# Opening loads in order of use on one queue, and parts of one bank for the mixers' small products, in a two-layer decoder trunk

## The chip, the cores and the metric

The kernel runs on one core of one Trainium2 chip. A core has five engines with instruction streams of their own: PE (TensorE, matrix products; its weight loads are listed apart as PEld), DVE (VectorE), ACT (ScalarE), POOL (GpSimd, used here to issue transfers) and SP (SyncE, which only issues transfers). An engine runs its stream in order; engines wait for one another by semaphores. A transfer that is issued on SP, ACT or POOL goes through that engine's queue, in order, and is issued only when the tile that it fills is free, so one that waits holds back all behind it. The metric is the device time of one execution in microseconds (us), lower is better. Times come as medians of several executions; a profile is one execution more, taken by the hardware profiler.

## The reference

Two layers over 256 tokens of width 1024, batch 1, float32, then a final RMS norm. Each layer is two half-step SwiGLU blocks around a token mixer; every one of the three has its own shift, scale and gate, computed from a vector c:

```
c_act = silu(c)
for l in 0, 1:
    mod = c_act @ w_ada[l] + b_ada[l]        # nine vectors of 1024: shift, scale, gate for each of three blocks
    h = rmsnorm(x, g[l,0]) * (1 + sc0) + sh0
    x = x + 0.5 * g0 * ((silu(h @ w_gate) * (h @ w_up)) @ w_down)          # inner width 2816
    h = rmsnorm(x, g[l,1]) * (1 + sc1) + sh1
    x = x + g1 * token_mix(h)
    h = rmsnorm(x, g[l,2]) * (1 + sc2) + sh2
    x = x + 0.5 * g2 * swiglu(h)             # a second set of weights
x = rmsnorm(x, final_g)
```

`token_mix` projects h to thirteen parts and joins three groups before an output projection: a gated MLP (gelu, a group norm, a causal 128x128 product), a differential attention with four heads (two softmax maps, one subtracted from the other), and a sparse attention with eight heads (compressed blocks of 32 tokens with a softmax over 15 of them, a selection of blocks, and a window).

## The kernel before

**Products.** x is held transposed as `xT`, 8 chunks k of 128 features by 256 tokens. A float32 product is made of three products of a shorter type: a weight tile `wst` (mostly 128x1024, 512 KB) is loaded by SP (L205), ACT rounds it to `wh` (L211), DVE takes the rest `wl = wst - wh` (L215), the activations are split likewise into a hi and a lo half of `h` (L279, L280), and PE adds wh by hi, wh by lo and wl by hi (L223, a helper that records all such products). `wst` has 5 buffers, `wh` and `wl` 6 each. PE has 8 banks of PSUM for results: 5 with tag "mm", 2 with tag "w", 1 with tag "st".

**Modulation.** w_ada is read in tiles `ast` of 128x1024 (512 KB, four buffers), loaded by POOL's queue (L181, and L374 in the opening). One DVE instruction multiplies a tile with the row `crow` = silu(c) and sums it into a column of 128 values (L192, in the opening L381). 16 tiles are due in the opening (scale and shift for each k); the other 128 are spread over the rest, and each must be summed before its block.

**The opening, `startup`.** The first SwiGLU starts with its first 7 column blocks of gate and up side by side: for every k a tile with 4 blocks (128x1024) and one with 3 (128x768) of `w_first`, products into 7 banks at once (`ps_fst`, 42 products per k). In the same loop stand the two `ast` sums for k+1, from which DVE makes `gs` (L383) and `mod` (L385), the scale and shift of one chunk, then `tn` (L276), and ACT and DVE make the halves of h. The first k is recorded in an order by hand for PE, DVE and ACT; the rest is laid out by a scheduler. In the whole loop the rest of the constants (`cst`, 706 KB, and `par`, 499 KB) and a small weight (`w2` from cmp_w2, 192 KB) are loaded on SP where the scheduler puts them. What follows is `ffn`: for the blocks 7 to 21 a gate and an up tile each (`ps_ws`), silu by ACT (`sg`, L344) times up by DVE (`a`, L349), then the down products (`ps_dn`), which DVE adds to `xT` (L332) and turns into `ut` (L294), the input of the mixer's first projections (`ps_wu`).

**The mixers.** `mix` runs a list of named steps, MIX_ORDER, whose order is PE's order; the other engines' orders are laid out by the scheduler, which puts an instruction where it sees its engine free. In the list of layer 0, `a` is `ada_step`: sum two tiles, load two. Projections (`ws_in`) take the two banks of tag "w"; so do the two products `xs_in` that come before them, and DVE copies half of these away (`dv`, L655) ahead of the first projection's use of the bank. Three small results take turns in the one bank "st": `ps_cs` (scores of the compressed blocks), `ps_ct` (their probabilities transposed) and `ps_da` (the norm of the differential attention).

Of the kernel before, what the change touches and what calls it, by code (L numbers as in the profile page):

```python
# [112 lines left out]
def trunk_kernel(ctx: ExitStack, tc: tile.TileContext, A, depth=DEPTH, nf=NF, fsplit=FSPLIT):  # L113
# [93 lines left out]

    def split(src, cols, mid=None):
        st = load(src, cols)
        wh = whp.tile([P, cols], F32R, name="wh", tag="wh")  # L210
        nc.scalar.activation(wh, st, AF.Copy)  # L211
# [151 lines left out]
    def startup(ns):  # L363
# [3 lines left out]
        nc.gpsimd.dma_start(crow, A["crow"])  # L367
        b1 = sm.tile([P, KD], F32, name="b1", tag="b1", bufs=1)

        def ada_load0(k):  # L370
            sts = []
            for m in (1, 0):
                st = adp.tile([P, D], F32, name="ast", tag="ast")
                nc.gpsimd.dma_start(st, A["w_ada"][0, m, k])  # L374
                sts.append(st)
            return sts

        def ada_sum0(k, sts):
            red = sm.tile([P, 2], F32, name="red", tag="red")
            for n, st in enumerate(sts):  # L380
                nc.vector.scalar_tensor_tensor(out=st, in0=st, scalar=1.0, in1=crow, op0=ALU.mult, op1=ALU.mult,  # L381
                                               accum_out=red[:, n:n + 1])
            nc.vector.scalar_tensor_tensor(out=gs[0][:, 0, k:k + 1], in0=red[:, 0:1], scalar=b1[:, k:k + 1],  # L383
                                           in1=lp(0, "ng")[:, k:k + 1], op0=ALU.add, op1=ALU.mult)
            nc.vector.tensor_add(mod[0][:, 0, k:k + 1], red[:, 1:2], lp(0, "bada")[:, k:k + 1])  # L385

        def first(k, mid=None):
            parts = []
            for f0, f1 in ((0, (ns + 1) // 2), ((ns + 1) // 2, ns)):
                if f1 > f0:  # L390
                    src = A["w_first"][k, :, f0 * 2 * P:f1 * 2 * P]
                    parts.append((f0, f1, *split(src, 2 * (f1 - f0) * P, None if f0 else mid)))
            return parts

        with tc.manual_schedule(engines={mybir.EngineType.PE, mybir.EngineType.DVE, mybir.EngineType.Activation}):
# [24 lines left out]
            ada_sum0(0, sts)  # L420
            rb = rms_bcast(rsqrt_tokens(st), in_psum=True)
            parts = first(0, lambda: h_chunk(0, 0, 0, rb))
        pss = []
        for f in range(ns):
            pool_, tag = (psm, "mm") if f < 5 else (psw, "w")
            pss.append(pool_.tile([P, 2 * T], F32, name="ps_fst", tag=tag))
        for k in range(KD):
            if k:
                parts = first(k)
            if k + 1 < KD:  # L430
                ada_sum0(k + 1, ada_load0(k + 1))
                h_chunk(0, 0, k + 1, rb)
            for f0, f1, wh, wl in parts:
                tiles = [(pss[f][:, e * T:(e + 1) * T], 2 * (f - f0) + e) for f in range(f0, f1) for e in range(2)]
                step = len(tiles) if k == 0 else 1
                for n0 in range(0, len(tiles), step):
                    for o, n in tiles[n0:n0 + step]:
                        s = slice(n * P, (n + 1) * P)
                        mm(o, wh[:, s], h[:, k, :T], start=(k == 0 and n % 2 == 0), stop=False)
# [695 lines left out]
```

## Time and profile before

| what | value |
|---|---|
| three runs | 1076.78, 1077.12, 1075.27 us; median 1076.78 |
| profiled execution | 1076.35 us, of which the span from first to last instruction 1074.4 us; mean granted clock of TensorE 0.982 |
| busy | PE 1028.0 us (96%), DVE 849.0 (79%), ACT 576.3 (54%), POOL 77.7 (7%) |
| transfers | 258.05 MB, 240 GB/s on average |
| first product of the opening | at 17.66 us |
| first of the products that follow it (`ps_ws`) | at 73.20 us |
| mixer of layer 0, first product to the first of the next block | 215.94 to 361.79 us |
| mixer of layer 1, the same | 737.32 to 877.02 us |

A median of executions is compared with a median. The profiled execution's time lies 1.95 us above its span, since the span counts from the first instruction to the last. PE's busy time counts overlapped products, so 96% is not 96% of its peak; the granted clock tells how fast it was allowed to run (1.00 is full speed, near 0.50 is half).

### The profile page before, as it was taken

The numbers are of one execution on the slowest core, as the hardware profiler recorded it, in microseconds if no ns is written. First come the engines' busy times: TensorE is split into PE (matmuls) and PEld (weight loads), VectorE is DVE, ScalarE is ACT, GpSimd is POOL, SyncE is SP. The second block draws the span as 40 slices with busy tenths as digits, with TensorE's granted clock in tenths as the row PEclk, the third lists the DMA queues.
The fourth block names the chain that finished last, engine by engine and source line by source line (L and its number), as shares of the span: only waits on it lengthen the run. The fifth ranks groups of instructions, "written<-read, shape, count | busy, mean of one in ns | idle before, by whom it ended". The sixth has DMA issues, their size and how long they took to land.

```text
span 1074.4 us, 19840 instructions
## 1 busy us (share of the span) xinstructions
PE 1028.0 (96%) x7684; PEld 948.5 (88%) x7684; DVE 849.0 (79%) x1589; ACT 576.3 (54%) x1022; POOL 77.7 (7%) x151
## 2 busy tenths in 40 slices
PE   7789999999898999999999999999998999999997
PEld 5689998888676999998899999889786799999986
DVE  5689989989994899965679999667987489655553
ACT  4355544565576755444565544455566676444441
POOL 2101111000100022100001111000000001000000
PEclk8899999999999999999999999999998999999999
DMA  9899998947620499986658999765632057756551
GB/s 361 301 327 328 390 365 308 366 132 249 228 95 21 157 388 408 404 274 174 192 159 308 409 408 368 249 189 176 237 133 67 1 177 299 229 181 184 170 154 40
DMA packets 73967, 258.05 MB, mean 240 GB/s; under 512 B 8337, under 2 KB 9745, under 8 KB 73873
## 3 DMA queue, kind: packets, MB, share of 16 engines
q1 hardware_dynamic: 52560, 180.17, 48.7%
q0 software_dynamic: 20880, 76.03, 19.0%
q8 instruction: 60, 0.98, 0.4%
q10 hardware_dynamic: 432, 0.58, 0.2%
q14 instruction: 35, 0.28, 0.1%
HBM read 255.70 MB, written 1.05 MB: 239 GB/s over the span
## 4 chain that ended last, share of the span: by engine, by line
PE 77%; DVE 11%; DMA 6%; ACT 3%; issue 2%; POOL 0%; DVEq 0%; ACTq 0%; POOLq 0%; SPq 0%
PE ps_ws L223 42%; PE ps_dn L223 23%; PE ps_out L223 4%; PE ps_wu L223 4%; DVE wl L215 3%; DMA ast<-in_w_ada_dram 2%; PE ps_y L223 1%; DMA wst<-in_w_first_dram 1%; PE ps_s L223 1%; ACT pn L541 1%; DVE rt L515 1%; DVE mx L536 1%; DMA wst<-in_w_in_vs_dram 1%; ACT wh L211 1%; DVE h L280 1%
## 5 line engine op out<-in xcount | busy, mean ns | idle before, releaser
L211 ACT ACTIVATE wh<-wst 128x1024 fp32r<-128x1024 f32 (+2 forms) x332 | 342.0, 1032 | 360.7 <-issue 129.7
L215 DVE TENSOR_TENSOR wl<-wst,wh 128x1024 fp32r<-128x1024 f32 (+2 forms) x332 | 392.6, 1187 | 117.6 <-ACT wh L211 115.7
L223 PE MATMUL ps_ws<-h,wh 128*128 128x256 f32 x2720 | 481.3, 281 | 4.0 <-DVE dv L655 1.7
L223 PEld LDWEIGHTS ps_ws<-h,wh 128*128 128x128 f32 x2720 | 416.3, 189 | 7.4 <-DVE dv L655 2.5
L223 PE MATMUL ps_ws<-h,wl 128*128 128x256 f32 x1360 | 382.0, 281 | 0.0
L223 PEld LDWEIGHTS ps_ws<-h,wl 128*128 128x128 f32 x1360 | 261.1, 192 | 0.0
L223 PE MATMUL ps_dn<-act,wh 128*128 128x512 f32 (+1 forms) x726 | 247.9, 390 | 0.0
L223 PE MATMUL ps_dn<-act,wl 128*128 128x256 f32 x704 | 197.6, 281 | 0.0
L223 PEld LDWEIGHTS ps_dn<-act,wh 128*128 128x128 f32 x726 | 134.8, 188 | 30.8
L192 DVE SCALAR_TENSOR_TENSOR ast<-ast,crow 128x1024 f32<-128x1024 f32 x128 | 156.8, 1226 | 1.6 <-DMA ast<-in_w_ada_dram 1.6
L223 PEld LDWEIGHTS ps_dn<-act,wl 128*128 128x128 f32 x704 | 133.1, 189 | 0.0
L181 POOL DMA_DIRECT2D ast<-in_w_ada_dram x128 | 68.0, 531 | 465.3 <-DVE ast L192 144.2
L223 PE MATMUL ps_wu<-ut,wh 128*128 128x258 f32 (+1 forms) x320 | 60.1, 286 | 0.8 <-DVE ut L294 0.8
L223 PE MATMUL ps_fst<-h,wh 128*128 128x256 f32 x224 | 42.1, 300 | 12.6 <-ACT h L279 12.6
L223 PEld LDWEIGHTS ps_wu<-ut,wh 128*128 128x128 f32 x320 | 49.9, 189 | 1.4 <-DVE ut L294 1.3
L223 PEld LDWEIGHTS ps_fst<-h,wh 128*128 128x128 f32 x224 | 36.5, 208 | 14.1 <-ACT h L279 13.8
L223 PE MATMUL ps_out<-y,wh 128*128 128x256 f32 x256 | 47.3, 286 | 0.4 <-DVE xT L332 0.4
L219 ACT ACTIVATE act<-a 128x256 fp32r<-128x256 f32 x88 | 35.6, 412 | 18.3 <-DVE a L349 17.0
L223 PE MATMUL ps_wu<-ut,wl 128*128 128x258 f32 x160 | 45.2, 283 | 0.0
L349 DVE TENSOR_TENSOR a<-ps_ws,sg 128x256 f32<-128x256 f32 x75 | 32.0, 427 | 14.8 <-PE ps_ws L223 14.8
L223 PEld LDWEIGHTS ps_out<-y,wh 128*128 128x128 f32 x256 | 39.8, 191 | 2.0 <-issue 1.0
L332 DVE SCALAR_TENSOR_TENSOR xT<-ps_dn,hg,xT 128x256 f32<-128x256 f32 x63 | 30.4, 482 | 12.6 <-PE ps_dn L223 11.5
(202 smaller groups left out, 1033.0 us busy)
## 6 DMA issues: line engine op xcount, KB each, us to landing
ast<-in_w_ada_dram POOLq DMA_DIRECT2D x144, 512.0 KB, 7.1
wst<-in_w_gate_dram SPq DMA_DIRECT2D x81, 512.0 KB, 5.7
wst<-in_w_up_dram SPq DMA_DIRECT2D x81, 512.0 KB, 6.0
wst<-in_w_down_dram SPq DMA_DIRECT2D x64, 512.0 KB, 4.4
wst<-in_w_in_ws_dram SPq DMA_DIRECT2D x28, 512.0 KB, 4.3
wst<-in_w_down_dram SPq DMA_DIRECT2D x32, 384.0 KB, 3.5
wst<-in_cmp_w_dram SPq DMA_DIRECT2D x16, 512.0 KB, 6.3
wst<-in_w_out_dram SPq DMA_DIRECT2D x16, 512.0 KB, 3.6
```

The lines of the kernel that those rows point to most:

```text
L181: nc.gpsimd.dma_start(st, A["w_ada"][l, m, c])
L192: nc.vector.scalar_tensor_tensor(out=st, in0=st, scalar=1.0, in1=crow, op0=ALU.mult, op1=ALU.mult, accum_out=reds[l, m][:, c:c + 1])
L211: nc.scalar.activation(wh, st, AF.Copy)
L215: last_wl[0] = nc.vector.tensor_sub(wl, st, wh.bitcast(F32))
L219: nc.scalar.activation(dst[:, :T], src, AF.Copy)
L223: nc.tensor.matmul(out, lhsT, rhs, start=start, stop=stop, skip_group_check=True)
L280: nc.vector.scalar_tensor_tensor(out=h[:, k, T:], in0=t, scalar=sh, in1=h[:, k, :T].bitcast(F32), op0=ALU.add, op1=ALU.subtract)
L332: nc.vector.scalar_tensor_tensor(out=xT[:, m, :], in0=ps[:, half * T:(half + 1) * T], scalar=hg[l][:, s, m:m + 1], in1=xT[:, m, :], op0=AL ...
L349: nc.vector.tensor_mul(a, pu, sg)
L515: nc.vector.tensor_mul(out, z, t)
L536: nc.vector.tensor_reduce(mx[:, :n], ps, axis=AX.X, op=ALU.max, negate=True)
L541: nc.scalar.activation(pt[:, g * w:(g + 1) * w], ps[:, g, :], AF.Exp, bias=mx[:, g:g + 1], accum_out=su[:, g:g + 1])
```

## The change

**Opening.** All loads of the opening go through SP's queue, in the order in which they are used: two of the four pieces of `xT` (the other two stay on ACT's queue), the first columns of `cst`, `crow`, then for each k the two `ast` tiles and the two `w_first` tiles, the `ast` tiles one k further ahead than before. The rest of `cst` and `par` is loaded after the last `w_first` tile. The two loads of the mixers that the scheduler had moved forward (`wsT` and `w2`) are tied behind the last `w_down` load before their mixer. Of a chunk, `xr` = xT times the norm is made by DVE for two chunks at once (L402), `gs` and `mod` by ACT (L391, L393), `tn` by ACT (L396), the hi half by ACT (L397) and the lo half by DVE (L398). The whole loop is recorded by hand for PE, DVE and ACT, and on PE the products of a tile go hi for all its blocks, then lo, then wl.

**Mixers.** The three tiles of the bank "st" become column ranges of one tile `small`. The first projection after `xs_in` takes a bank of tag "mm" (`ws_next`). The seven `a` steps of layer 0 are gone; instead the tiles still loaded are summed and four are loaded at the mixer's start, four summed and four loaded after the early projections, and the last four summed after `lam_exp`. The casts of two constants (`identb`, `negb`) are tied behind the last `wl` before the mixer.

```diff
@@ MIX_ORDER, layer 0 (the seven "a" are taken out, the rest stands in the same order)
-k.1 dp.0 dp.1 ds.0 c.0 dx.0 k.0 ds.1 dx.1 c.1 v dr.0 q.0 ch dr.1 ns.0 a co do.0 do.1 nx.0 a cs.0 dn q.1 a q.2 go df ns.1
+k.1 dp.0 dp.1 ds.0 c.0 dx.0 k.0 ds.1 dx.1 c.1 v dr.0 q.0 ch dr.1 ns.0 co do.0 do.1 nx.0 cs.0 dn q.1 q.2 go df ns.1
...
@@ startup
-        nc.gpsimd.dma_start(crow, A["crow"])
+        dma(cst[:, :P], A["cst"][:, :P])
+        dma(crow, A["crow"])
...
-                nc.gpsimd.dma_start(st, A["w_ada"][0, m, k])
+                dma(st, A["w_ada"][0, m, k])
...
+        def h_first(k, red):
+            nc.scalar.activation(gs[0][:, 0, k:k + 1], red[:, 0:1], AF.Identity, scale=lp(0, "ng")[:, k:k + 1],
+                                 bias=gb[:, k:k + 1])
+            nc.scalar.activation(mod[0][:, 0, k:k + 1], red[:, 1:2], AF.Identity, bias=lp(0, "bada")[:, k:k + 1])
+
+            t = tp.tile([P, T], F32, name="tn", tag="t1k")
+            nc.scalar.activation(t, xr[k // 2][:, k % 2], AF.Identity, scale=gs[0][:, 0, k:k + 1], bias=mod[0][:, 0, k:k + 1])
+            nc.scalar.activation(h[:, k, :T], t, AF.Copy)
+            nc.vector.tensor_sub(h[:, k, T:], t, h[:, k, :T].bitcast(F32))
+
+        def xr_pair(n, rp):
+            t = up.tile([P, 2, T], F32, name="xr", tag="u")
+            nc.vector.tensor_mul(t, xT[:, 2 * n:2 * n + 2], rp[:, None, :].to_broadcast([P, 2, T]))
+            xr.append(t)
...
+            for k in range(KD):
+
+                f0, f1, st0 = raw[0]
+                wh, wl = split_raw(st0, 2 * (f1 - f0) * P)
+                parts = [(f0, f1, wh, wl)]
+                h_first(k, red)
+                for f0, f1, st0 in raw[1:]:
+                    parts.append((f0, f1, *split_raw(st0, 2 * (f1 - f0) * P)))
+                if k + 1 < KD:
+                    raw = first_load(k + 1)
+                    if k % 2 == 0 and k // 2 + 1 < KD // 2:
+                        xr_pair(k // 2 + 1, rp)
+                    red = ada_sum0(k + 1, sts)
+                    if k + 2 < KD:
+                        sts = ada_load0(k + 2)
...
-        dma(cst[:, P:], A["cst"][:, P:])
-        dma(par[:, npar0:], A["par"][:, npar0:])
+        with tc.issue_after(last_ld[0].ins):
+            dma(cst[:, P:], A["cst"][:, P:])
+            dma(par[:, npar0:], A["par"][:, npar0:])
@@ mix
+        ada_sum(len(loaded))
+        ada_load(4)
         pse = [ws_u(WI[l, 0])]
...
-        ada_sum(len(loaded))
+        ada_sum(4)
+        ada_load(4)
+
+        small = [pst.tile([P, 512], F32, name="ps_small", tag="st")]
...
-        nc.sync.dma_start(wsT, A["gm_w_s"][l])
+        with tc.issue_after(last_dn[0].ins):
+            nc.sync.dma_start(wsT, A["gm_w_s"][l])
...
+        def ws_next(n):
+            behind_xs[0] -= 1
+            return ws_in(WI[l, n], psm, "mm") if behind_xs[0] >= 0 else ws_in(WI[l, n])
...
         lam_exp(gelu)
+        ada_sum(4)
...
-            dst = pst.tile([P, 8], F32, name="ps_da", tag="st")
+            dst = small[0][:, 384:392]
...
-            ps = pst.tile([P, 60], F32, name="ps_cs", tag="st")
+            ps = small[0][:, 256 + (j % 2) * 64:316 + (j % 2) * 64]
...
-            ps = pst.tile([P, T], F32, name="ps_ct", tag="st")
+            ps = small[0][:, :T]
```

Three places show how the instructions stand. The first is SP's queue from the program's first load. Before (POOL's queue carried `crow` and all `ast` tiles beside it):

```order
L366 DMA xT<-in_xT_dram 128x512 x2
L404 DMA cst<-in_cst_dram 128x128
L205 DMA wst<-in_w_first_dram 128x1024
L205 DMA wst<-in_w_first_dram 128x768
L205 DMA wst<-in_w_first_dram 128x1024
L205 DMA wst<-in_w_first_dram 128x768
L205 DMA wst<-in_w_first_dram 128x1024
L443 DMA cst<-in_cst_dram 128x1412
L444 DMA par<-in_par_dram 128x998
L205 DMA wst<-in_w_first_dram 128x768
```

Now:

```order
L366 DMA xT<-in_xT_dram 128x512 x2
L367 DMA cst<-in_cst_dram 128x128
L368 DMA crow<-in_crow_dram 128x1024
L375 DMA ast<-in_w_ada_dram 128x1024 x2
L205 DMA wst<-in_w_first_dram 128x1024
L205 DMA wst<-in_w_first_dram 128x768
L375 DMA ast<-in_w_ada_dram 128x1024 x2
L205 DMA wst<-in_w_first_dram 128x1024
L205 DMA wst<-in_w_first_dram 128x768
```

The two large pieces of constants stood between two weight tiles of the third k, and now stand behind the last of the eighth; the `ast` tiles stand one k ahead of the weights in the same queue.

The second place is the loop of the opening on DVE, one k of it. Before:

```order
L381 SCALAR_TENSOR_TENSOR ast,red<-ast,crow 128x1024
L280 SCALAR_TENSOR_TENSOR h<-tn,mod_102,h 128x256
L381 SCALAR_TENSOR_TENSOR ast,red<-ast,crow 128x1024
L383 SCALAR_TENSOR_TENSOR gs_104<-red,b_115,par 128x1
L385 TENSOR_TENSOR mod_102<-red,par 128x1
L215 TENSOR_TENSOR wl<-wst,wh 128x1024
L276 SCALAR_TENSOR_TENSOR tn<-xT,gs_104,rp 128x256
L215 TENSOR_TENSOR wl<-wst,wh 128x768
```

Now, and on ACT beside it:

```order
L215 TENSOR_TENSOR wl<-wst,wh 128x1024
L398 TENSOR_TENSOR h<-tn,h 128x256
L215 TENSOR_TENSOR wl<-wst,wh 128x768
L402 TENSOR_TENSOR xr<-xT,rp 128x512
L386 SCALAR_TENSOR_TENSOR ast,red<-ast,crow 128x1024 x2
```

```order
L213 ACTIVATE wh<-wst 128x1024
L391 ACTIVATE gs_104<-red,gb,par 128x1
L393 ACTIVATE mod_102<-red,par 128x1
L396 ACTIVATE tn<-xr,mod_102,gs_104 128x256
L397 ACTIVATE h<-tn 128x256
L213 ACTIVATE wh<-wst 128x768
```

The two sums of a chunk now stand behind both `wl` of the chunk before, and both `gs`, `mod` and `tn` are ACT's; the row with `xr` is there for k = 0, 2 and 4 alone. Behind the last k, DVE's `a` of all 7 blocks stand ahead of the next `wl`, where four `wl` stood ahead of them before.

The third place is DVE in the mixer of layer 0, from the copies of `dv`. Before, four `wl` and then the copies, and the sums later, between the softmax pieces:

```order
L215 TENSOR_TENSOR wl<-wst,wh 128x1024 x4
L655 COPY dv<-ps_xs 128x256 x2
L767 TENSOR_REDUCE mu<-vg 128x8
L215 TENSOR_TENSOR wl<-wst,wh 128x1024
L572 TENSOR_TENSOR nlam<-le 128x1
```

```order
L858 TENSOR_SCALAR gate<-gate,cst 128x8 x2
L192 SCALAR_TENSOR_TENSOR ast,red_3451<-ast,crow 128x1024 x2
L515 TENSOR_TENSOR rt_3337<-ps_ws,cst 128x256
L515 TENSOR_TENSOR rt_3339<-ps_ws,cst 64x256 x2
L822 SCALAR_TENSOR_TENSOR hid<-th,ps_h_3343 128x60
L525 TENSOR_TENSOR qn<-rt_3337,rt_3339 128x256
L822 SCALAR_TENSOR_TENSOR hid<-th,ps_h_3350 128x60
L192 SCALAR_TENSOR_TENSOR ast,red_3451<-ast,crow 128x1024
```

Now three sums stand among them, and none later:

```order
L215 TENSOR_TENSOR wl<-wst,wh 128x1024
L192 SCALAR_TENSOR_TENSOR ast,red_2709<-ast,crow 128x1024 x3
L692 COPY dv<-ps_xs 128x256
L160 TENSOR_TENSOR mod_102<-red_2709,par 128x8
L215 TENSOR_TENSOR wl<-wst,wh 128x1024
L692 COPY dv<-ps_xs 128x256
```

Of the eight sums of this mixer, the other five moved further ahead: four into the end of the down products before it, one between its first projections.

More of the change, by code (lines that the diff above doesn't have):

```diff
@@ L171, in trunk_kernel @@
     todo, loaded, reds, done = [], [], {}, set()
-    last_wl = [None]
+    last_wl, last_ld = [None], [None]
     def ada_load(n, after=None):
@@ L382, in ada_sum0 @@
                                                accum_out=red[:, n:n + 1])
[L383 to L393, printed above, removed]
+            return red
+        def h_first(k, red):
[10 more added lines that the diff above has]
+            xr.append(t)
+        xr = []
         with tc.manual_schedule(engines={mybir.EngineType.PE, mybir.EngineType.DVE, mybir.EngineType.Activation}):
@@ L403, in startup @@
             sts = ada_load0(0)
-            dma(cst[:, :P], A["cst"][:, :P])
-            nc.vector.tensor_scalar_add(b1, lp(0, "bada")[:, KD:2 * KD], 1.0)
+            raw = first_load(0)
+            nc.vector.scalar_tensor_tensor(out=gb, in0=lp(0, "bada")[:, KD:2 * KD], scalar=1.0,
+                                           in1=lp(0, "ng")[:, :KD], op0=ALU.add, op1=ALU.mult)
             st = psw.tile([P, NI], F32, name="ps_st", tag="w")
@@ L419, in startup @@
             nc.scalar.activation(warm, ones, AF.Sqrt)
[L420 to L439, printed above, removed]
-                        mm(o, wh[:, s], h[:, k, T:], start=False, stop=False)
-                    for o, n in tiles[n0:n0 + step]:
-                        mm(o, wl[:, n * P:(n + 1) * P], h[:, k, :T], start=False, stop=(k == KD - 1))
@@ L443, in startup @@
-        dma(cst[:, P:], A["cst"][:, P:])
-        dma(par[:, npar0:], A["par"][:, npar0:])
+            red = ada_sum0(0, sts)
+            rp = rms_bcast(rsqrt_tokens(st), in_psum=True)
+            xr_pair(0, rp)
+            sts = ada_load0(1)
+            pss = []
+            for f in range(ns):
+                pool_, tag = (psm, "mm") if f < 5 else (psw, "w")
+                pss.append(pool_.tile([P, 2 * T], F32, name="ps_fst", tag=tag))
+            for k in range(KD):
[12 more added lines that the diff above has]
+                        sts = ada_load0(k + 2)
+                for f0, f1, wh, wl in parts:
+                    tiles = [(pss[f][:, e * T:(e + 1) * T], 2 * (f - f0) + e) for f in range(f0, f1) for e in range(2)]
+                    for wx, hs, first_, last_ in ((wh, slice(0, T), True, False), (wh, slice(T, 2 * T), False, False),
+                                                  (wl, slice(0, T), False, True)):
+                        for o, n in tiles:
+                            mm(o, wx[:, n * P:(n + 1) * P], h[:, k, hs], start=(first_ and k == 0 and n % 2 == 0),
+                               stop=(last_ and k == KD - 1))
```

37 lines of the change are left out of this document (21 added, 16 removed).

## The prediction

> **What bounds the kernel now.** I read the page first, then the chain of waits that ended last, then the opening by windows, then both mixers. The chain (share of the span by what it waited for, and its longest pieces: start, length, what):
>
> ```profile
> PE 77%; DVE 11%; DMA 6%; ACT 3%; issue 2%; POOL 0%; DVEq 0%; ACTq 0%; POOLq 0%; SPq 0%
> ...
> 3.48 14.32 DMA ast<-in_w_ada_dram
> 24.39 11.34 DMA wst<-in_w_first_dram
> 53.85 5.67 DMA wst<-in_w_gate_dram
> 64.15 5.68 DMA wst<-in_w_up_dram
> 73.20 81.88 PE ps_ws L223 x720
> 155.09 60.91 PE ps_dn L223 x351
> ...
> 344.42 17.53 PE ps_out L223 x144
> ...
> 675.32 62.07 PE ps_dn L223 x351
> ...
> 859.65 17.54 PE ps_out L223 x144
> ```
>
> From 73.2 us on, long stretches are PE alone, at 81.88/720 = 0.1137 us a product. Before that the chain is transfers. So PE bounds the large blocks, and the opening is a stage of its own with another limit. Its windows, and the large blocks behind it (stretch, its length, then busy time of PE, PEld, DVE, ACT and POOL, the granted clock, the share of the DMA engines and GB/s):
>
> ```profile
> 20.00:30.00 10.00, 9.37 (x77) 9.17 (x76) 8.35 (x15) 1.84 (x4) 1.06 (x2) 0.93 1.02 409
> 30.00:40.00 10.00, 2.65 (x12) 2.66 (x13) 4.78 (x9) 4.69 (x6) 1.06 (x2) 0.58 0.78 307
> 60.00:73.00 13.00, 10.48 (x86) 9.89 (x85) 10.17 (x16) 6.64 (x10) 1.06 (x2) 1.00 1.01 367
> 73.00:216.00 143.00, 142.80 (x1073) 135.57 (x1074) 135.03 (x224) 76.58 (x114) 19.14 (x36) 1.00 0.94 344
> ```
>
> In 20 to 30 the DMA engines are full; in 30 to 40 PE is busy 2.65 of 10 us at a clock of 0.58. The timeline of PE (start, length, in brackets the idle time ahead and who ended it) shows when the opening's products start, the hole, and what follows them:
>
> ```profile
> 17.66 0.80 PE L223 MATMUL ps_fst<-h,wh 128*128 128x256 f32 x2 [2.40 <-ACT h L279]
> 37.34 1.01 PE L223 MATMUL ps_fst<-h,wh 128*128 128x256 f32 x3 [7.98 <-ACT h L279]
> 71.60 0.28 PE L223 MATMUL ps_fst<-h,wl 128*128 128x256 f32 x1
> 73.20 0.50 PE L223 MATMUL ps_ws<-h,wh 128*128 128x256 f32 x2 [1.33 <-DVE a L349]
> ```
>
> The hole names ACT's h, but the chain shows that a weight transfer of 11.34 us from 24.39 stood ahead of it: the 1.2 MB of constants between the weights of the third k. The 42 x 8 = 336 products need 38.2 us; they take 17.66 to 71.9.
>
> **The opening, worked out.** Loads first. The GB/s of forty 2 us slices from 0 to 80, then one queue alone (766 to 776) and two together (10 to 34):
>
> ```profile
> GB/s 18 164 370 404 421 420 414 406 407 413 416 409 419 392 406 408 406 409 294 16 195 340 274 217 330 296 268 338 356 373 360 383 367 301 371 393 401 289 29 305
> ...
> DMA packets 1138, 3.92 MB, mean 392 GB/s; under 512 B 127, under 2 KB 127, under 8 KB 1137
> ...
> DMA packets 2867, 9.83 MB, mean 410 GB/s; under 512 B 318, under 2 KB 418, under 8 KB 2866
> ```
>
> One queue carries what two did, so moving `ast` to SP costs no rate. [...] The first slices give 1.1 MB by 6 us and 0.8 MB per 2 us after. In order of use, xT, small constants and `crow` (1.70 MB) are in by 7.5 us, the first two `ast` by 8.6 and 9.9, the first weights by 11.1 and 12.1. A k is 1.97 MB, 4.8 us at 0.41 MB/us.
>
> Durations (group: busy, mean ns, idle before), and behind them the first step of the norm in ACT's timeline:
>
> ```profile
> L381 DVE SCALAR_TENSOR_TENSOR ast<-ast,crow 128x1024 f32<-128x1024 f32 x16 | 19.5, 1222 | 3.0 <-DMA ast<-in_w_ada_dram 2.6 <-ACT warm L419 0.3
> L215 DVE TENSOR_TENSOR wl<-wst,wh 128x1024 fp32r<-128x1024 f32 x12 | 14.6, 1222 | 1.5 <-ACT wh L211 1.5
> L211 ACT ACTIVATE wh<-wst 128x1024 fp32r<-128x1024 f32 x12 | 12.7, 1059 | 17.8 <-PE ps_fst L223 7.0 <-DMA wst<-in_w_up_dram 6.2 <-DMA wst<-in_w_first_dram 3.9
> L215 DVE TENSOR_TENSOR wl<-wst,wh 128x768 fp32r<-128x768 f32 x8 | 7.6, 954 | 2.2 <-ACT wh L211 2.2
> L211 ACT ACTIVATE wh<-wst 128x768 fp32r<-128x768 f32 x8 | 6.7, 843 | 14.7 <-DMA wst<-in_w_first_dram 14.4 <-PE ps_fst L223 0.2
> L279 ACT ACTIVATE h<-tn,mod 128x256 fp32r<-128x256 f32 x8 | 4.0, 495 | 3.6 <-DVE tn L276 3.6
> L280 DVE SCALAR_TENSOR_TENSOR h<-tn,mod,h 128x256 fp32r<-128x256 f32 x8 | 3.9, 484 | 7.4 <-ACT h L279 7.4
> L344 ACT ACTIVATE sg<-ps_fst 128x256 f32<-128x256 f32 x7 | 2.0, 406 | 0.0
> L412 DVE TENSOR_TENSOR sq<-xT 128x512 f32<-128x512 f32 x2 | 1.3, 685 | 0.0
> ...
> 12.28 0.26 ACT L256 ACTIVATE rs<-ps_st,eps 128x2 f32<-128x2 f32 x1 [1.58 <-PE ps_st L223]
> ```
>
> In the new order one chain goes round once per k: the two sums are ready; ACT does `gs`, `mod` (not in the trace; the nearest row is 0.26 us for 128x2, I take 0.25 each), `tn` and the hi half (0.5 each, by L279): 1.5; then ACT's second `wh` 0.84; then DVE's second `wl` 0.95; then the next two sums 2.45. That is 5.75 us, and 0.69 more (`xr`, by the row of 128x512) for k = 0, 2, 4. DVE alone needs 1.22 + 0.48 + 0.95 + 2.45 = 5.1, transfers 4.8, PE 42 x 0.1137 = 4.8, so the chain through both engines is the longest. Start: first sums done near 11.1; the norm, held to 12.28 before while xT shared the engines with `ast`, is ready about a us sooner; first h near 13.9. DVE then does two `wl`, a lo half, `xr` and two sums, so the second k's sums are ready near 18.7. The eighth's: 18.7 + 6 x 5.75 + 2 x 0.69 = 54.6. PE's last k starts 1.5 later and takes 4.8: end near 60.9, against 71.9.
>
> Then the tail loses something. Before, four `wl` stood ready when the blocks began. Now three `sg` are left at 60.9 (3 x 0.41), then `wh` 1.06, then `wl` 1.22, in that order on their engines: `ps_ws` runs without pause from about 64.4, against 73.20: **-8.8 us**. PE stands 3.5 us. What such a stand costs is in the mixer's rows:
>
> ```profile
> 284.30 1.22 PE L223 MATMUL ps_s<-kn,qn 128*128 128x256 f32 x2 [2.18 <-DVE qn L525]
> ...
> 284.00:288.00 4.00, 3.70 (x8) 2.25 (x9) 3.10 (x6) 0.00 (x0) 0.00 (x0) 0.57 0.22 89
> ```
>
> After 2.18 us idle the next 4 us had a clock of 0.57: 0.43 x 4 = 1.7 us lost. I take **+1.7** (0, as in 60 to 73, where 2.5 us idle in small pieces left the clock at 1.00, to 2.7, if the loss grows with the pause). [...] Bounds of the opening: 4 us shorter if ACT's small steps cost 0.5 more per k and hand-overs add up; 11 if DVE's 5.1 alone sets the pace.
>
> **Down to the mixer.** PE then sets the pace, so an earlier start carries through, if DVE can follow:
>
> ```profile
> 84.00:95.00 11.00, 11.00 (x100) 11.00 (x99) 11.00 (x20) 6.87 (x12) 1.60 (x3) 1.00 0.85 277
> 128.00:139.00 11.00, 11.00 (x100) 11.00 (x99) 11.00 (x18) 5.77 (x9) 2.12 (x4) 1.00 1.01 389
> ```
>
> DVE is full there. From 73 to 216 it has 143 - 135.03 = 8.0 us free. It gets four `wl` that stood ahead (4.9) and four sums of the mixer (4.9), and gives one or two `wl` (1.2 to 2.4) on to the mixer: a little over. I take **+1.0** (0 to 4.9).
>
> **The mixer of layer 0.** In the chain, from the end of the down products to the end of the output's: 216.00 to 361.95, 145.95 us; in layer 1, 737.39 to 877.19, 139.80, with the same products and no sums. So some 6.15 is to be had. The sums (L192) as a group, windows, and two rows of PE's timeline:
>
> ```profile
> L192 DVE SCALAR_TENSOR_TENSOR ast<-ast,crow 128x1024 f32<-128x1024 f32 x8 | 9.7, 1218 | 1.0 <-DMA ast<-in_w_ada_dram 1.0
> ...
> 242.00:256.00 14.00, 13.79 (x118) 13.60 (x118) 13.72 (x30) 7.45 (x12) 0.00 (x0) 1.00 0.72 234
> ...
> 292.00:296.00 4.00, 3.16 (x21) 3.09 (x21) 4.00 (x13) 2.87 (x16) 0.00 (x0) 0.80 0.58 194
> ...
> 219.18 0.39 PE L223 MATMUL ps_wu<-ut,wh 128*128 128x256 f32 x1 [0.42 <-DVE ut L294]
> ...
> 241.74 0.51 PE L223 MATMUL ps_ws<-h,wh 128*128 128x256 f32 x2 [1.70 <-DVE dv L655]
> ```
>
> DVE is full in both windows, and all 8 sums stood about the second, with 1.0 us of waits for their tiles. Four leave the mixer (4 x 1.22), and those waits go. The first projection no longer waits for `dv` (1.70), but three sums now stand ahead of its second `wl`: 3.7 us, which takes about as much back. `qn` keeps about its time, since more `wl` stand ahead of it where sums stood; after it DVE has three sums and as many `wl` less. The idle time and lost clock round it are 2.18 + 1.7 and, in 292 to 296, 0.84 + 0.8: 5.5 in all; I take half, -2.8, as the sums are gone and the `wl` are not. Against it, the `wsT` product (128x512, 0.69) now stands ahead of the last `ut`, for which PE waits already: **-2.1** in sum (-6.15 to +1).
>
> The parts of one bank I cost at nothing. The instructions of the changed program that write and read `small` wait for one another as they did through the three tiles. [...] Layer 1: no sums are there, 0 (+-1).
>
> Sum: -8.8 + 1.7 + 1.0 - 2.1 = -8.2. From the profiled execution, 1076.35 (its span 1074.4 and 1.95 around it): 1068.15. The median of the runs lies 0.43 above it, so **1068.6 us**.
>
> **The rivals.** A: the mixer gives its whole 6.15 and the clock does not fall: -8.8 + 1.0 - 6.15 = -14, 1062.8. For it: layer 1 does the same products in that time; against it: three sums ahead of `dv`. B: the opening gives half, because hand-overs lengthen the round from 5.75 to 6.4, as 7 x 0.65 = 4.6 us, and the rest as forecast: 1073.2. For it: ACT and DVE take turns, each wait on the path. C: the blocks become bound by DVE. It was at 11.00 of 11.00 with four `wl` in hand; without them PE waits out the whole 4.9, the four sums at the end of the down products hold the last `ut` by 4.9 more, and the mixer gives nothing: -7.1 + 9.8 = +2.7, 1079.5. It decides from the point where DVE's added work is over 7.1 us beyond its free 8.0; I count at most 2.5 beyond, which speaks against it. D: the change does nothing to be measured: the round is as long as before's 54/8 = 6.8 us and the mixer's waits stay: 1076.8. Against it: the hole of 7.98 us cannot be there once the constants stand last.
>
> **How the numbers follow.** Forecast 0.58, A 0.18, B 0.12, C 0.07, D 0.05. What can be told from no change here is 0.2%, 2.2 us. Faster: forecast, A and B, 0.88; same 0.05; slower 0.07. Range: 1061.5 to 1073.5, from A to B.
>
> **What would show it.** Right: first `ps_fst` near 14, a round of 5.8 us with DVE and ACT in turn, no hole at 30 to 40, `ps_ws` from about 64, a clock below 1 just behind that; the mixer of layer 0 in about 144 us, no wait for `dv`, and a shorter one for `qn`. Wrong: idle time of DVE in the opening that is ended by `ast` or `wst` transfers; PE waits for `wl` between 64 and 207; a wait for the last `ut` of over 2 us.

## The result and the profile after

| | before | changed |
|---|---|---|
| median of the runs | 1076.03 us (1074.75 to 1077.12) | 1064.12 us (1061.90 to 1066.46) |
| ratio | | 0.9887, 95% interval 0.9862 to 0.9911 |
| span of the profiled execution | 1074.4 us | 1062.7 us |
| first of the products `ps_ws` that run on without pause | 73.20 us | 63.07 us |
| first mixer, end of the down products to end of the output's | 145.95 us | 144.5 us |
| second mixer, the same | 139.80 us | 137.8 us |

1.1% faster, about 12 us. The forecast was 1068.6; the measured time lies 4.5 us below it and inside the stated range. The chain of waits that ended last in the changed kernel, its shares and its long pieces (start, length, what):

```profile
PE 75%; DVE 15%; ACT 5%; issue 3%; DMA 2%; DVEq 0%; SPq 0%; ACTq 0%
...
5.16 7.89 DMA wst<-in_w_first_dram
17.95 2.38 DVE ast L386 x4
23.38 2.38 DVE ast L386 x4
26.20 6.64 DMA wst<-in_w_first_dram
34.84 2.38 DVE ast L386 x4
...
63.07 83.37 PE ps_ws L223 x718
146.43 40.86 PE ps_dn L223 x236
...
334.25 17.54 PE ps_out L223 x144
...
665.16 62.07 PE ps_dn L223 x351
...
847.48 17.54 PE ps_out L223 x144
```

Transfers had 6% of the chain and have 2%; in the opening the pairs of sums on DVE have taken their place, 5.4 or 6.0 us apart. One weight transfer, from 26.20 to 32.84, still stands on the chain: it landed just before ACT came to its tile, and that round is no longer than the others. Laid against the pieces of before, the 11.7 us between the two profiled executions are found so: 10.1 at the first `ps_ws`; 1.5 of them given back by the end of that block (83.37 us where it was 81.88); 1.5 gained in the first mixer (the output's products end at 351.79, 10.16 ahead; the down products ended 8.6 ahead); nothing from there to 727.23; 2.0 gained in the second mixer; 0.4 given back at the end.

The opening by windows, in the changed kernel (stretch, length, busy PE, PEld, DVE, ACT, POOL, granted clock, DMA share, GB/s), and two smaller ones behind it:

```profile
20.00:30.00 10.00, 10.00 (x87) 10.00 (x86) 8.76 (x14) 6.62 (x11) 0.00 (x0) 1.00 1.03 407
30.00:40.00 10.00, 8.80 (x74) 8.41 (x73) 8.76 (x14) 6.46 (x12) 0.00 (x0) 1.00 0.94 328
...
60.20:63.61 3.41, 1.45 (x10) 1.03 (x9) 2.60 (x5) 3.02 (x6) 0.00 (x0) 1.00 1.02 408
63.61:67.02 3.41, 3.41 (x18) 3.41 (x18) 3.18 (x3) 2.78 (x3) 0.00 (x0) 0.50 0.91 323
```

The window 30 to 40, in which PE was busy 2.65 us at a clock of 0.58, is at 8.80 and 1.00. A fall of the clock comes behind the opening, from 63.61 to 67.02: 0.5 x 3.41 = 1.7 us, about what the block lost. PE's timeline shows the pauses ahead of it, and three waits at the start and in the middle of the first mixer:

```profile
15.76 3.70 PE L223 MATMUL ps_fst<-h,wh 128*128 128x256 f32 x16 [1.92 <-ACT h L397]
33.25 2.10 PE L223 MATMUL ps_fst<-h,wh 128*128 128x256 f32 x16 [0.81 <-ACT h L397]
55.56 2.10 PE L223 MATMUL ps_fst<-h,wh 128*128 128x256 f32 x16 [0.38 <-ACT h L397]
62.12 0.50 PE L223 MATMUL ps_ws<-h,wh 128*128 128x256 f32 x2 [1.51 <-ACT wh L213]
63.07 0.50 PE L223 MATMUL ps_ws<-h,wh 128*128 128x256 f32 x2 [0.45 <-ACT wh L213]
210.57 0.90 PE L223 MATMUL ps_wu<-ut,wh 128*128 128x258 f32 x2 [0.59 <-ACT ut L293]
233.98 0.38 PE L223 MATMUL ps_ws<-h,wl 128*128 128x256 f32 x1 [1.85 <-DVE wl L215]
275.18 3.68 PE L223 MATMUL ps_s<-kn,qn 128*128 128x256 f32 x6 [0.92 <-DVE qn L548]
```

The wait of 1.70 for `dv` became one of 1.85 for the second `wl`; the wait for `qn` went from 2.18 to 0.92; the last `ut` costs 0.59 where it cost 0.42. One round of the opening on DVE, and ACT's two small steps in it:

```profile
29.41 1.22 DVE L386 SCALAR_TENSOR_TENSOR ast<-ast,crow 128x1024 f32<-128x1024 f32 x1
...
31.70 1.22 DVE L215 TENSOR_TENSOR wl<-wst,wh 128x1024 fp32r<-128x1024 f32 x1
33.23 0.42 DVE L398 TENSOR_TENSOR h<-tn,h 128x256 fp32r<-128x256 f32 x1 [0.31 <-ACT h L397]
33.97 0.96 DVE L215 TENSOR_TENSOR wl<-wst,wh 128x768 fp32r<-128x768 f32 x1 [0.31 <-ACT wh L213]
34.84 1.22 DVE L386 SCALAR_TENSOR_TENSOR ast<-ast,crow 128x1024 f32<-128x1024 f32 x1
```

```profile
30.67 0.39 ACT L391 ACTIVATE gs<-red,gb,par 128x1 f32<-128x1 f32 x1 [1.49 <-DVE ast L386]
31.82 0.30 ACT L393 ACTIVATE mod<-red,par 128x1 f32<-128x1 f32 x1 [0.76 <-DVE ast L386]
```

From 29.41 to 34.84 is a round of 5.43 us, in which DVE waits twice for ACT and never for a transfer. That is the chain through both engines, as forecast, at 5.43 instead of 5.75 us.

### The profile page after: what moved, and what is told of

It reads as the page before. It is cut to its first block, busy times and chain, and to the rows that moved or that the text cites. A ratio compares the mean times of both kernels' runs of the same rounds, so it can differ in the third digit from the quotient of the medians.

```text
span 1062.7 us, 19847 instructions
## 1 busy us (share of the span) xinstructions
PE 1025.2 (96%) x7684; PEld 946.3 (89%) x7684; DVE 847.9 (80%) x1569; ACT 584.6 (55%) x1046; POOL 68.8 (6%) x134
## 4 chain that ended last, share of the span: by engine, by line
PE 75%; DVE 15%; ACT 5%; issue 3%; DMA 2%; DVEq 0%; SPq 0%; ACTq 0%
PE ps_ws L223 41%; PE ps_dn L223 21%; PE ps_out L223 4%; PE ps_wu L223 4%; DVE wl L215 3%; DVE rt L538 2%; DMA wst<-in_w_first_dram 1%; DVE ast L386 1%; PE ps_s L223 1%; DVE mx L559 1%; DVE ast L192 1%; PE ps_y L223 1%; ACT wh L213 1%; ACT pn L564 1%; DVE h L280 1%
## 5 line engine op out<-in xcount | busy, mean ns | idle before, releaser
L220 DVE TENSOR_TENSOR act<-a,act 128x256 fp32r<-128x256 f32 x88 | 36.1, 416 | 0.2 <-ACT act L219 0.2
L223 PE MATMUL ps_out<-y,wl 128*128 128x256 f32 x128 | 36.2, 283 | 0.0
```

The costliest lines, as they stand in the source:

```text
L220: nc.vector.tensor_sub(dst[:, T:], src, dst[:, :T].bitcast(F32))
L223: nc.tensor.matmul(out, lhsT, rhs, start=start, stop=stop, skip_group_check=True)
```

## The experiments

Times are medians with the ratio to before and its 95% interval; lengths of pieces come from one profiled execution each.

**The two parts apart.** `opening_alone` is the changed kernel with the mixers of before; `mixers_alone` is the kernel before with the changed mixers. Both have the ties of the two mixer loads and of the casts.

```diff
 opening_alone, against the changed kernel
-k.1 dp.0 dp.1 ds.0 c.0 dx.0 k.0 ds.1 dx.1 c.1 v dr.0 q.0 ch dr.1 ns.0 co do.0 do.1 nx.0 cs.0 dn q.1 q.2 go df ns.1
+k.1 dp.0 dp.1 ds.0 c.0 dx.0 k.0 ds.1 dx.1 c.1 v dr.0 q.0 ch dr.1 ns.0 a co do.0 do.1 nx.0 a cs.0 dn q.1 a q.2 go df ns.1
...
-        ada_sum(len(loaded))
-        ada_load(4)
...
-            return ws_in(WI[l, n], psm, "mm") if behind_xs[0] >= 0 else ws_in(WI[l, n])
+            return ws_in(WI[l, n])
...
-            dst = small[0][:, 384:392]
+            dst = pst.tile([P, 8], F32, name="ps_da", tag="st")
...
```

> The changed kernel with its mixers put back to the ones before (the seven a steps, three tiles in the bank st, the first projection in a bank of tag w); the opening and the ties of the two mixer loads and of the casts stay as changed. Theory (the parts add): ps_ws begins at 63 us as in the changed kernel, 10.1 earlier than before; 1.5 of it is lost again to a low clock at 64 to 68; the first mixer lasts 145.9 and the second 139.8 us as before; span 1074.4 - 8.6 = 1065.8. Rival (the mixers' gains of 1.5 and 2.0 come from where the earlier start puts them, not from their own change): the mixers last 144.4 and 137.8, span 1062.5.

> The kernel before with the change in the mixers alone (and the ties of loads and casts). Theory: the opening ends where it did, ps_ws at 73.2; first mixer 144.4, second 137.8; span 1074.4 - 3.5 = 1070.9. Rival (the mixers' change brings nothing of its own): span within 1 us of 1074.4.

Measured: `opening_alone` 1067.29 us, 0.9902 (0.9879 to 0.9925). Its chain:

```profile
62.47 83.10 PE ps_ws L223 x718
145.56 60.92 PE ps_dn L223 x351
333.74 17.54 PE ps_out L223 x144
...
664.65 62.07 PE ps_dn L223 x351
...
848.75 17.54 PE ps_out L223 x144
```

The first mixer lasts 144.8 us and the second 139.6. So most of the gain is the opening's: 0.98 of 1.13 per cent by the ratios. The span was 1063.9, 1.9 under the theory's sum: the first mixer, with one fall of the clock less than before, was 1.1 us shorter, and `ps_ws` began 0.6 us earlier than expected.

`mixers_alone` 1075.48 us, 0.9986 (0.9966 to 1.0005): by the runs, nothing that can be told. Three rows of its PE timeline:

```profile
73.74 0.51 PE L223 MATMUL ps_ws<-h,wh 128*128 128x256 f32 x2 [2.10 <-DVE a L349]
222.52 0.39 PE L223 MATMUL ps_wu<-ut,wh 128*128 128x258 f32 x1 [1.74 <-ACT ut L293]
247.46 0.38 PE L223 MATMUL ps_ws<-h,wl 128*128 128x256 f32 x1 [1.84 <-DVE wl L215]
```

The theory's sum, 1070.9, was wrong by 2.7 (the span was 1073.6). Of this 2.2 us were lost ahead of the mixers: PE waited 2.10 us ahead of `ps_ws` (1.33 before), and the clock in 74 to 78 was 0.57 (1.00 before), so that the down products ended at 218.2 instead of 216.0. That part is not the mixers'. The first mixer lasted 145.2 us instead of the expected 144.4: the last `ut` holds PE for 1.74 us here, against 0.59 in the changed kernel, and the clock in 224 to 228 behind it was 0.58. That the sums and the `wsT` product ahead of it on DVE are what makes it late is read from the order and not tested. The second mixer lasted 137.5, with one fall of the clock where there were two before.

**Constants last.** The kernel before with one edit:

```diff
...
-        dma(cst[:, P:], A["cst"][:, P:])
-        dma(par[:, npar0:], A["par"][:, npar0:])
+        with tc.issue_after(last_ld[0].ins):
+            dma(cst[:, P:], A["cst"][:, P:])
+            dma(par[:, npar0:], A["par"][:, npar0:])
```

> The kernel before with one edit: the rest of cst and par (1.2 MB) is loaded on SP behind the last weight of the opening. Theory (the change gained by two things, the constants out of the way and the loop in lockstep): the hole at 29 to 37 us shrinks from 8.0 to at most 4, ps_ws begins near 69, span about 1070.5. Rival 1 (the constants were all of it): ps_ws at 63 to 64, span 1064 to 1066. Rival 2 (the loop of DVE and ACT was all of it): ps_ws moves by less than 1 us.

1070.62 us, 0.9945 (0.9915 to 0.9976). PE's timeline, and a line of the chain:

```profile
31.95 0.51 PE L223 MATMUL ps_fst<-h,wh 128*128 128x256 f32 x2 [2.20 <-ACT h L279]
50.75 0.50 PE L223 MATMUL ps_fst<-h,wh 128*128 128x256 f32 x2 [2.33 <-ACT h L279]
```

```profile
67.24 81.60 PE ps_ws L223 x720
```

Two loads put last make the hole of 7.98 us one of 2.20 and bring `ps_ws` 6.0 us forward (the theory had 4), 6 of the 10 that the whole opening brings. The other 4 are the rest of the opening's change: the loop by hand, the one queue, and the two mixer loads (`wsT`, `w2`) that no longer stand in it. No run parts these three. The two rivals that had it all in one cause fall.

**The bank behind `xs_in`.** The changed kernel with its first projection back in a bank of tag "w":

```diff
-            return ws_in(WI[l, n], psm, "mm") if behind_xs[0] >= 0 else ws_in(WI[l, n])
+            return ws_in(WI[l, n])
```

> The changed kernel, with the first projection behind xs_in back in a bank of tag w. Theory: PE waits for the second dv copy, which stands behind one wl more than the wait of 1.85 us in the changed kernel ends at; that wait grows to 3 to 4.5 us, the first mixer and the time lengthen by 1.5 to 3 us. Rival (the second wl is what is waited for, the bank does not matter): no change within 0.5 us.

1063.94 us, 0.9874 (0.9852 to 0.9896): no change. PE's timeline, and a line of the chain:

```profile
230.43 0.39 PE L223 MATMUL ps_ws<-h,wh 128*128 128x256 f32 x1 [0.85 <-DVE dv L692]
231.64 0.39 PE L223 MATMUL ps_ws<-h,wl 128*128 128x256 f32 x1 [0.70 <-DVE wl L215]
```

```profile
62.37 81.75 PE ps_ws L223 x718
```

One wait of 1.85 is now two of 0.85 and 0.70, 1.55 together. The expectation of 3 to 4.5 us was wrong: PE waits for the same stretch of DVE either way, and by the runs the bank does not matter so long as three sums stand there. One execution leaves room for a little: without its clock falls the first mixer lasted 142.0 us, against 141.1 and 140.7 in the two of the changed kernel.

**Parts or tiles in the bank "st".** The changed kernel with three tiles again in place of `small`:

```diff
...
-            ps = small[0][:, 256 + (j % 2) * 64:316 + (j % 2) * 64]
+            ps = pst.tile([P, 60], F32, name="ps_cs", tag="st")
...
-            ps = small[0][:, :T]
+            ps = pst.tile([P, T], F32, name="ps_ct", tag="st")
```

> The changed kernel with the bank of small products as three tiles again, ps_cs, ps_ct and ps_da, in place of one tile with parts. Theory (its parts wait for one another by bank, so that they take turns as the three tiles did): both mixers as in the changed kernel without clock falls, 141.1 and 135.6 to 136.4 us, within 0.5. Rival (the parts let the scores of the second pair of heads begin before the rows of the first are read): mixers 1 to 2 us longer, with a new wait ahead of ps_cs.

1063.60 us, 0.9863 (0.9832 to 0.9895): the time of the changed kernel. The wait ahead of the scores is 0.46 us, as in the changed kernel; the mixers lasted 144.2 and 140.7 us, of which the granted clock accounts for 5.1 us each (the sum over 2 us windows of what it lacked to 1), so 139.1 and 135.6 without. For the second that is as expected; for the first it is 2 us below the 141.1 of the changed kernel, outside the half us that I had allowed, but not on the rival's side. The parts bring nothing that shows.

**The round of the opening.** In the loop, the two sums of the next chunk ahead of the second `wl`:

```diff
+                if k + 1 < KD:
+                    red = ada_sum0(k + 1, sts)
                 for f0, f1, st0 in raw[1:]:
                     parts.append((f0, f1, *split_raw(st0, 2 * (f1 - f0) * P)))
...
-                    red = ada_sum0(k + 1, sts)
```

> The changed kernel with one edit: in the opening's loop DVE makes the two sums of the next chunk ahead of the second wl of this one. Theory (the round of 5.43 us is the chain through DVE and ACT: two sums, gs, mod, tn, hi half, second wh, second wl): the second wh and wl leave the chain, DVE's own work of 5.0 us sets the round (5.7 with xr), seven rounds end 2 to 2.7 us earlier, the last ps_fst at 57.5 to 58 instead of 60.2, ps_ws the same amount earlier. Rival (the transfers or PE, 4.8 us each, already set most of it): under 1 us, and idle time of DVE ended by transfers. Rival 2: the second tile's products wait for its wl, which now comes 2.4 us later: PE shows a new pause in each round and nothing is gained.

1062.22 us, 0.9872 (0.9843 to 0.9902). Its round on DVE, first and last row, and ACT and PE behind the loop:

```profile
31.03 1.22 DVE L386 SCALAR_TENSOR_TENSOR ast<-ast,crow 128x1024 f32<-128x1024 f32 x1
...
35.84 1.22 DVE L386 SCALAR_TENSOR_TENSOR ast<-ast,crow 128x1024 f32<-128x1024 f32 x1
```

```profile
57.79 1.06 ACT L213 ACTIVATE wh<-wst 128x1024 fp32r<-128x1024 f32 x1 [1.21 <-DMA wst<-in_w_gate_dram]
58.90 0.58 PE L223 MATMUL ps_ws<-h,wh 128*128 128x256 f32 x1 [2.82 <-ACT wh L213]
```

The round is 4.81 us, and the last product of the opening ends near 56.1 instead of 60.6, earlier than the 57.5 to 58 expected: the chain of sums, `mod`, `tn`, `h`, `wh`, `wl` is what set it, and the rivals fall. But PE then waits 2.82 us for `wh`: ACT has the seven silu until 56.6, and then waits 1.21 us more for the first gate tile, whose load stands behind the 1.2 MB of constants in the queue. The clock is at half from 58.8 to 65.6, some 3.4 us of lost time: more than half of the 4.5 us goes there, and the down products begin at 144.37, 2.1 us ahead of the changed kernel.

**The tail.** The first gate tile behind the opening is split ahead of the silu products, the first up tile behind four of them; both are thereby also loaded ahead of the constants:

```diff
...
-        wh, wl = split(src, KD * P)
+        wh, wl = pre7.pop(0) if pre7 else split(src, KD * P)
...
+            gu7 = [load(A["w_gate"][0, 0, ns], KD * P), load(A["w_up"][0, 0, ns], KD * P)]
+            pre7.append(split_raw(gu7[0], KD * P))
+            out = [swiglu_mul(ps[:, :T], ps[:, T:], None, None, up, "u") for ps in pss[:4]]
+            pre7.append(split_raw(gu7[1], KD * P))
+            out += [swiglu_mul(ps[:, :T], ps[:, T:], None, None, up, "u") for ps in pss[4:]]
...
-        return [swiglu_mul(ps[:, :T], ps[:, T:], None, None, up, "u") for ps in pss]
+        return out
```

> The changed kernel with one edit: wh and wl of the first gate tile behind the opening are made ahead of the seven silu and their products, and those of the first up tile behind four of them. Theory (the tail is the order on ACT and DVE): the pauses of 1.5 and 0.45 us ahead of ps_ws go to under 0.5, ps_ws begins without pause near 60.5 instead of 63.1, and the clock does not fall behind it; the down products begin 2.5 us earlier than in a run of the changed kernel in which the clock held, 4.2 than in one in which it fell. Rival (a free bank or the table load of 1.28 us sets it): ps_ws moves by under 1 us.

1062.03 us, 0.9870 (0.9839 to 0.9901). The pauses are gone, `ps_ws` begins at 60.59 and the clock holds, as expected. But the block takes longer:

```profile
60.59 84.80 PE ps_ws L223 x720
```

84.80 us at a granted clock of 1.00, where `dv_bank_back` took 81.75: a product comes every 0.1178 us instead of 0.1133. More of that below.

**The sums of the first mixer, late.** The last four tiles are loaded behind the fourth q and summed behind the third `nsa_out`:

```diff
...
         lam_exp(gelu)
-        ada_sum(4)
...
+        def late_load():
+            seen = sm.tile([P, 1], F32, name="seen", tag="seen", bufs=1)
+            ada_load(4, nc.gpsimd.tensor_copy(seen, qt[3][:, 0:1]))
...
+            "al": late_load, "a": lambda: ada_sum(4),
```

> The changed kernel with the last four w_ada tiles of the first mixer loaded behind the fourth q and summed behind the third nsa_out, instead of in front of its projections. Theory (three sums ahead of the second wl cost the wait of 1.85 us and put DVE behind up to qn; after 300 us DVE has time): the wait at 234 goes, qn's waits shrink, the mixer's length without clock falls goes from 141.1 to 138 to 139. Rival (the sums are paid wherever they stand, since the softmax pieces behind 300 are a chain of their own that they lengthen): 141 to 142. Rival 2 (the waits go, but others in the same stretch take their place): 140.5 to 141.

> The kernel with the last four sums late, profiled once more. Theory (the slow pace of its first block, 84.9 us against 81.8, is a chance of the execution): the first block may take 81.8 us this time, or 83.4 with a clock fall. Rival (the pace belongs to the program, to where its code or its tiles lie): 84.9 again, and the down products 62.2 again.

1067.97 us, 0.9902 (0.9864 to 0.9940), and 1067.37 the second time: slower than the changed kernel by the medians, though the intervals overlap. The wait for the second `wl` is gone and 0.21 us is left of the one for `qn`, but behind 300 us, where the sums now stand on DVE (311 to 317), PE waits longer for the softmax chain (rows of the first of the two):

```profile
311.59 0.70 PE L223 MATMUL ps_s<-kn,qn 128*128 128x512 f32 x1 [1.64 <-ACT pn L564]
316.22 0.44 PE L976 MATMUL ps_t<-cst,pn 128*128 128x128 f32 x2 [1.06 <-ACT pn L564]
319.34 0.44 PE L223 MATMUL ps_y<-pt,vsw 128*64 128x256 f32 x2 [1.39 <-ACT pn L564]
```

In the changed kernel the first two are 1.36 and 0.57 us. All of PE's pauses between 305 and 325 come to 5.7 us here and 5.1 there. Behind them the clock was at half from 320.5 to 330.7. The mixer lasted 145.1 and 145.5 us, longer than the 144.5 of the changed kernel; without the falls it would be 140.0 and 138.7 against 141.1, so the waits saved are there, but in these two executions the clock lost behind 300 took more. That the late sums alone bring these falls is not shown: `dv_bank_back`, without them, had one from 320.4 to 327.2. The other loss is the slow pace again, in both executions, in the first block and its down products: 84.91 us each time, against 81.75 in `dv_bank_back`, and 62.19 against 60.92 in `opening_alone`.

**All three**, the sums ahead, the early split and the late sums together:

> The three edits together on the changed kernel: sums ahead of the second wl in the opening, the first gate and up tile split early, the last four sums of the first mixer late. Theory: the gains add, 2.3 + 2.5 + 2.5 = 7.3 us against the changed kernel, give or take a clock fall of 1.7: median 1056 to 1058. Rival (the tail's gain is the same time as the loop's, since ACT is the one that is late): 4 to 5 us, 1059 to 1060.

1063.02 us, 0.9858 (0.9816 to 0.9899): no better than the changed kernel by anything that can be told. The theory of added gains was wrong. The late sums and the slow pace (the block's 694 products in 82.00 us, 0.1182 each) took it back, and in the opening a transfer had become the last thing waited for, as ACT's timeline shows:

```profile
60.16 1.06 ACT L213 ACTIVATE wh<-wst 128x1024 fp32r<-128x1024 f32 x1 [2.46 <-DMA wst<-in_w_gate_dram]
```

That is the second gate tile of the blocks, which now stood behind the 1.2 MB of constants. So in the last version the late sums were left out, the up tile was split behind two silu products, and the constants were moved behind the third up tile of the blocks:

```diff
...
+            if l == 0 and w == 0 and f == f0 + 2:
+                with tc.issue_after(last_ld[0].ins):
+                    nc.sync.dma_start(cst[:, P:], A["cst"][:, P:])
+                    nc.sync.dma_start(par[:, npar0:], A["par"][:, npar0:])
```

> The changed kernel with three edits in the opening: the sums ahead of the second wl, the first gate tile split ahead of the silu products and the first up tile behind two of them, and the rest of the constants loaded behind the third up tile of the blocks instead of ahead of the first but one. Theory (with the loop at 4.9 us a round the tail was held by the order on ACT and then by the constants in front of the gate tile): ps_fst ends near 56, ps_ws follows without a pause of over 0.5 us, the down products begin 56 + 82 = 138 us, or 141 at the slow pace, instead of 146.4; median 1055 to 1059. Rival (transfers now bound the opening, 4.8 us a round, and its debt is paid in the first blocks): pauses ahead of wst of 2 us and more between 56 and 80, median 1060 to 1062.

**1055.89 us, 0.9791 (0.9770 to 0.9813)**: 2.1% under the kernel before, and 8.8 us under the changed one as it ran beside it (`changed_again`, 1064.65). A window of its opening, a row of PE and one of its chain:

```profile
20.00:30.00 10.00, 10.00 (x90) 10.00 (x90) 10.00 (x16) 6.08 (x11) 0.00 (x0) 1.00 1.03 407
```

```profile
55.36 0.50 PE L223 MATMUL ps_ws<-h,wh 128*128 128x256 f32 x2 [0.39 <-DVE a L349]
```

```profile
55.36 81.88 PE ps_ws L223 x720
```

PE, DVE and the DMA engines are full at once in the opening, and the block follows with a pause of 0.39 us and no fall of the clock.

**The changed kernel once more**, unaltered:

> The changed kernel, unaltered, profiled once more. In the ten profiles so far a stall of 1.5 to 2.2 us is followed by a half clock in some and not in others, and the products of the first block come every 0.1133 us in some and every 0.1178 in others. Theory (both are chances of one execution): the same program shows another set of such places, so that the second mixer lasts 137.8 or 139.5 us and the first block 81.7, 83.4 or 84.8 us, while the waits themselves (1.5 and 0.45 ahead of ps_ws, 1.85 for wl) repeat to 0.1 us. Rival (they belong to the program): the same places, the second mixer 137.8 and the first block 83.4 again.

Its profiled execution took 1061.72 us, a further one 1067.59. The waits repeat (1.50 and 0.45 ahead of `ps_ws`, 1.82 for the second `wl`). The block took 83.36 us with a low clock from 63.9 to 67.3, the second mixer 137.6 again; but the first mixer lasted 142.3 us instead of 144.5: the clock fell behind the wait for `wl` as before, but not behind the one for `qn`. So of the places, one of four changed from one execution to the next, and neither side had it whole.

## Why the prediction came out as it did

**The opening's limit** was right: the loads in order of use remove the hole, one queue carries the rate (407 GB/s at 20 to 30), and the chain through DVE and ACT sets the round. `sums_ahead` shows the last of these by taking two links out of the chain.

**Its size** was made of errors that cancel. The first h was forecast at 13.9, and PE's first product came at 15.76. Two steps failed there, and they end together. The transfers at the start were taken too early: the first `ast` tile is waited for until 10.57 (forecast 8.6) and the first weights until 13.07 (forecast 11.1), and `gs` stands behind their `wh` in ACT's order. And the norm was not "ready about a us sooner": its reciprocal stands behind the first two sums in DVE's order, so `xr` begins at 13.88.

```profile
13.07 1.06 ACT L213 ACTIVATE wh<-wst 128x1024 fp32r<-128x1024 f32 x1 [1.13 <-DMA wst<-in_w_first_dram]
13.88 0.69 DVE L402 TENSOR_TENSOR xr<-xT,rp 128x512 f32<-128x512 f32 x1 [0.78 <-PE rp L264]
```

The round was forecast at 5.75 and measured 5.43: `gs` is not in the chain, since it needs the first sum alone and runs beside the second (30.67 above), and pieces overlap by up to 0.1 us where they join. `tn` was longer than taken (0.60), the hi half shorter (0.42). The end of `ps_fst` was forecast at 60.9 and measured at 60.6: the late start and the shorter rounds cancel, and that the end was met is luck. In the tail, `ps_ws` was forecast at 64.4 and came at 63.07. Here I had put three silu, `wh` and `wl` one behind the other with PE idle for 3.5 us. PE was idle for 1.51 and 0.45, since the three silu ran from 60.19 to 61.12, partly beside the last products, and the blocks' first products need `wh` alone.

**The clock term**, +1.7, came in with 1.7 in the profiled execution, but not as a rule. The same pauses, 1.49 to 1.51 and 0.44 or 0.45 us, were followed by a low clock in the changed kernel (both times), `opening_alone` and `three_tiles`, and by a clock of 1.00 in `dv_bank_back` and `late_sums` (both times). The traces show what parts the four from the three. In the profiled execution of the changed kernel the clock falls to 0.50 behind the opening at 63.61 and in the mixers at 234.28, 275.24 and 817.95 us, each time for 3.41 us, and the last three lie 50, 62 and 221 times 3.413 us behind the first, as on a grid. Where the grid lies differs from one execution to the next (a boundary at 63.61 here, at 61.00 and 64.42 in `dv_bank_back`). In the four, one stretch of the grid held most of the pauses: PE was busy for 1.45 to 1.83 us of it, and the next stretch ran at half clock (60.20 to 67.02 above). In the three, a boundary divided the pauses, no stretch had less than 2.07 us, and the clock held, as here in `dv_bank_back`:

```profile
57.59:61.00 3.41, 2.32 (x21) 2.13 (x19) 2.50 (x7) 2.36 (x8) 0.00 (x0) 1.00 1.03 412
61.00:64.42 3.42, 2.55 (x19) 2.33 (x20) 2.36 (x3) 2.23 (x3) 0.00 (x0) 1.00 1.00 385
```

By this count, four of seven, it is about an even chance, and the expected price is half of what I took. PE's busy time in a stretch does not settle it everywhere: 1.71 us in 239.71 to 243.12 of the kernel before was followed by a clock of 1.00. In the first mixer of the changed kernel one pause of 1.85 us was followed by a fall: PE was busy for 1.55 us in 230.87 to 234.28, and the clock was 0.50 from 234.28 to 237.69. Ahead of the fall at 275.24 PE was busy for 2.01 us in 271.83 to 275.24.

**The blocks**, +1.0 for a DVE without four `wl` in hand: nothing. Without a clock fall the block took 81.75 us in `dv_bank_back`, which also starts without that stock, and 81.88 before. That is why rival C had no hold: its first 4.9 us was no loss at all. Its second half is real, but small: the last `ut` at 0.59, and at 1.74 in `mixers_alone`. Between 64 and 207 us PE shows no wait, for `wl` or anything else.

**The first mixer**, -2.1 forecast, -1.5 measured, with 3.4 us of lost clock in both. The wait for `dv` moved to the second `wl` at the same price, as forecast; the one for `qn` shrank; the clock fell twice, as before. The bank of parts: nothing, as forecast (1063.60 us with three tiles, 1064.12 with the parts). That the parts wait for one another as the tiles did shows at 310.42, where the scores wait 0.46 us for `pct`, which reads another part; with three tiles this wait is 0.46 us too.

**The second mixer**, forecast 0, measured -2.0. Of this 1.7 is one fall of the clock less. With the same bank choice there, `sums_ahead` has 139.3 us and `late_sums` 139.6, both with 3.4 us of lost clock; `loop_and_tail` has 137.8 with 1.7. Without the falls every version lies between 135.6 and 136.4, before and after the change. So this part of the gain was not the change's.

The forecast of -8.2 against some 12 is thus made of: opening 1.3 better, no loss in the blocks 1.0, second mixer 2.0, the rest within 0.6 us each. The measured time lies nearer to rival A's 1062.8 than to the forecast, but A had it by the wrong way: the mixer did not give its 6.15. Rivals B and D fall with the round of 5.43 us and the hole that is gone.

## What to carry to other kernels

Cost an opening as a round: list its links across all engines, not the busiest engine's sum, and look for the one link that can leave the chain by a swap of two instructions. When a round gets shorter, go on to the handover behind it in the same step: here less than half of the loop's 4.5 us was left at the down products until the silu order and the constants in the queue were moved too. And where a stretch has pauses of one to two us on PE, look at the granted clock before reading a difference of 1.7 us between two executions as an effect of the edit: here a clock of 0.50 for 3.41 us cost that much.

## What was not expected of the hardware

The products of the first block come every 0.1133 us in some programs and every 0.1178 in others at a granted clock of 1.00, and the later blocks every 0.1178 in all of them (113.07 us for 960). `late_sums` was slow in both of its executions and the changed kernel fast in both, so it seems to go with the program; but `early_split` and `three_tiles` were slow in the block and not in its down products. It is worth 3.1 us in the block and 1.3 in the down products, more than most edits tried here. What decides it was not found.

A pause of 1.5 to 2.2 us on PE was followed by a half clock in some executions and not in others, at a cost of 1.7 us (63.61 to 67.02 in the changed kernel) or a multiple of it (5.1 us from 320.5 to 330.7 in `late_sums`). Behind the opening the half clock came in the four executions in which PE was busy for 1.45 to 1.83 us of one stretch of 3.41 us, and not in the three in which no stretch had less than 2.07. The single executions of one program scatter by 2 to 9 us (1063.21 to 1065.13 for `dv_bank_back`, 1061.90 to 1066.46 for the changed kernel, 1055.67 to 1064.57 for all three edits together).
